# A decoder trunk's beginning: who asks for the first blocks, in what pieces, and how sums over partitions are taken

## The chip, the core and the metric

The kernel runs on one core of a Trainium2 chip. The core has a matrix engine (TensorE), two elementwise engines (VectorE, ScalarE), a general one (GpSimd) and SyncE, which here only asks for transfers. Sixteen DMA engines move data between the chip's main memory and the core's on-chip memory. The metric is the device time of one execution in microseconds, a median over runs. A trace of one profiled execution tells when each instruction began and ended.

## The reference

A trunk of two layers over a sequence of 1024 tokens with 1024 features, all in float32. The first layer normalises each token by the root mean square of its features, multiplies by `w_in_a` (1024 x 2560), applies a short causal convolution and two gates to the first 1280 columns, runs a linear recurrence over time, multiplies by the SiLU of the other 1280 columns, and projects back by `w_out_a`. The second layer is a multi-head latent attention (8 heads, causal) with its own projections. A last normalisation gives the output. Of this the change touches two kinds of work: the start of the first projection, and two of the normalisations' sums.

```
h = rms_norm(x, norm_a)          # y = x * rsqrt(mean(x*x) + eps) * g
u = h @ w_in_a                   # 1024 x 1024 by 1024 x 2560
...
return rms_norm(x, final_norm)
```

## The kernel before, in words

Features lie on the 128 partitions and tokens along the free dimension, so x is eight blocks (`k` = 0 to 7) of 128 features by 1024 tokens, and a product with a weight matrix adds eight matmuls over `k` into one bank of PSUM (128 x 512 values: one of 128 output columns, one half of the tokens).

Float32 products are made from rounded parts. `hl` (lines 80 to 83) writes `hi`, a copy rounded to the type fp32r, on ScalarE (L82), and `lo = src - hi` on VectorE (L83). `mm3` (lines 113 to 116) then issues three matmuls: hi·hi (L114), weight hi by data lo (L115), weight lo by data hi (L116). A float32 matmul without this splitting is possible as well; in the trace it is two instructions in place of one.

The normalisation is taken behind the product: x is multiplied by the gain while it is split (`xsplit`, L261 on ScalarE and L262 on VectorE), and the factor of each token is applied to the product later (`byr`, L162). That factor needs the sum of x*x over all features: `squares(k)` squares block `k` on ScalarE (L277 for block 0, L279 for the others) and adds it into `accp` on VectorE (L158, the last with L156). `accp` then holds 128 partial sums for each token; a matmul with a matrix of ones (`onesd`) sums them over the partitions (L140, in `rstd`), and `newton` (L148 to L151) makes the reciprocal root.

The beginning (lines 285 to 338) goes thus. Nine matmuls of ones by ones (`NWARM`, L287) keep TensorE working while the first data come. Within `manual_schedule` the instructions of SyncE, ScalarE and VectorE are executed in the order in which they are written; TensorE's order is made by a planner, which may put a matmul that it expects to be ready ahead of one that waits. SyncE asks for the vectors (`vec`: gains, biases and so on, L128), the first half of x's block 0, four blocks of the first weight column group `wina[0]`, the second half of x's block 0, four blocks of `wina[10]` (the gate's columns), and then whole blocks of x (L254 for x, L266 for weights). The raw weights have two buffers, so the second four blocks of each group are asked for when the first have been split. For each `k`, x is split, four groups of three matmuls follow (two column groups by two halves of tokens), and the squares of the block before are added (`SQL` = 1 block late). Before block 4 the second weights are split. When all blocks are through, the sums over partitions follow for the two halves, and the rest of the softplus (`step`, small VectorE operations) with them. Behind the block the loop over ten channel tiles begins, in which the planner orders all engines.

The end (lines 992 to 1058) makes the last projection in three chunks of tokens (512, 256, 256). For each of eight output blocks it multiplies, adds the residual (L1036), squares on ScalarE (L1038, L1041), and adds into `acc` (L156, L158). The sum of a chunk over partitions (`final`, L1005) and its normalisation and store (L1008, L1009) are written behind the second output block of the next chunk. The last chunk sums in its own way (L1044, L1045). Tiles with the tag `sq` have two buffers there.

Of the kernel before, what the change touches and what calls it, by code (L numbers as in the profile page):

```python
# [9 lines left out]
F32 = mybir.dt.float32  # L10
F32R = mybir.dt.float32r
# [7 lines left out]
D = 1024  # L19
# [25 lines left out]
PG1 = 1  # L45
CHUNKS = ((0, 512), (512, 256), (768, 256))
FINAL = ((0, 2, "sync"), (2, 4, "scalar"), (4, 6, "sync"), (6, 8, "scalar"))
NWARM = 9
SQL = 1
GADD = ()  # L50
NWA = 7
# [6 lines left out]
def trunk(tc, xT, wina, vecs, wgate, wouta, winc, wuk, wuv, wuq, wuqr, woutb, rope, outT):  # L58
# [12 lines left out]
    def nm(s):  # L71
        uid[0] += 1
        return f"{s}_{uid[0]}"
# [7 lines left out]
    def hl(src, hi, lo):  # L81
        A.activation(out=hi, in_=src, func=AF.Copy)  # L82
        V.tensor_tensor(out=lo, in0=src, in1=f(hi), op=ALU.subtract)  # L83
# [39 lines left out]
    def hs(h):  # L123
        return slice(h * HW, (h + 1) * HW)


    vec = con.tile([P, NVEC], F32, name="vec")
    nc.sync.dma_start(out=vec, in_=vecs)  # L128
    tiny = con.tile([P, 1], F32, name="tiny")
    V.memset(tiny, 1e-30)  # L130
    atab = con.tile([P, 1], F32, name="atab")
# [2 lines left out]
    onesr = con.tile([P, P], F32R, name="onesr")  # L134
    V.tensor_copy(out=onesr, in_=onesd)

    def rstd(acc_half, out, ps, inv, y, u, parts=None):

        if parts is None:
            T.matmul(out=ps, lhsT=onesd, rhs=acc_half, start=True, stop=True)  # L140
        else:
            hl(acc_half, *parts)
            T.matmul(out=ps, lhsT=onesr, rhs=parts[0], start=True, stop=False)
            T.matmul(out=ps, lhsT=onesr, rhs=parts[1], start=False, stop=True)
        newton(out, ps, inv, y, u)

    def newton(out, ps, inv, y, u):
        A.activation(out=y, in_=ps, func=AF.Abs_reciprocal_sqrt, scale=inv)  # L148
        A.activation(out=u, in_=y, func=AF.Square)
        V.scalar_tensor_tensor(out=u, in0=ps, scalar=inv, in1=u, op0=ALU.mult, op1=ALU.mult)  # L150
        V.scalar_tensor_tensor(out=out, in0=u, scalar=-3.0, in1=y, op0=ALU.add, op1=ALU.mult)  # L151
# [26 lines left out]
    def tt(dt=F32):  # L178
        return ta.tile([P, HW], dt, tag="t", bufs=14, name=nm("t"))

    def pst():
        return psp.tile([P, HW], F32, tag="ps", name=nm("ps"))
# [68 lines left out]
    def xload(k, c=slice(0, S)):  # L251
        if len(xrs) == k:
            xrs.append(page(F32))
        nc.sync.dma_start(out=xrs[k][:, c], in_=xT[:, k, c])  # L254
# [6 lines left out]
        A.activation(out=xh, in_=xrs[k][:, c], func=AF.Copy, scale=g)  # L261
        V.scalar_tensor_tensor(out=xl, in0=xrs[k][:, c], scalar=g, in1=f(xh), op0=ALU.mult, op1=ALU.subtract)  # L262

    def wraw(src, k0):
        raw = wp.tile([P, 4 * P], F32, tag="wr", bufs=2, name=nm("wr"))
        nc.sync.dma_start(out=raw, in_=src[:, k0 * P:(k0 + 4) * P])  # L266
        return raw

    def wsplit(raw, ks):
        hi = wp.tile([P, 4 * P], F32R, tag="wh", bufs=4, name=nm("wh"))  # L270
        lo = wp.tile([P, 4 * P], F32R, tag="wl", bufs=4, name=nm("wl"))
        hl(raw, hi, lo)
        ks += [(hi[:, k * P:(k + 1) * P], lo[:, k * P:(k + 1) * P]) for k in range(4)]

    def squares(k):
        if k == 0:
# [10 lines left out]
        T.matmul(out=warm[:, 0:P], lhsT=onesd, rhs=onesd, start=True, stop=True)  # L287
    rb = accp
    with tc.manual_schedule(engines={_E.SP, _E.Activation, _E.DVE}):
        A.activation(out=atab, in_=onesd[:, 0:1], func=AF.Abs_reciprocal_sqrt)  # L290
        sp = softplus()

        def step(n):
            for _ in range(n):
                next(sp, None)

        xload(0, hs(0))
        r = [wraw(wina[0], 0)]
        xload(0, hs(1))
        r.append(wraw(wina[NCT], 0))  # L300
        xload(1)
        xload(2)
        xload(3)
        step(SPN[0])
        xsplit(0, hs(0))
        wsplit(r[0], wx)
        xsplit(0, hs(1))
        wsplit(r[1], wg)
        r = [wraw(wina[0], 4), wraw(wina[NCT], 4)]
        for k in range(4, NKT):  # L310
            xload(k)
        ps0 = [pst() for _ in range(4)]

        def products(k):
            for i in range(4):
                mm3(ps0[i], (wx, wg)[i // 2][k], (xs[k][0][:, hs(i % 2)], xs[k][1][:, hs(i % 2)]), k == 0, k == NKT - 1)

        products(0)
        done = 0
        for k in range(1, NKT):  # L320
            xsplit(k)
            step(SPN[1])
            if k == 3:
                wsplit(r[0], wx)
                wsplit(r[1], wg)
            products(k)
            while done <= k - SQL:
                squares(done)
                step(SPN[1])
                done += 1  # L330
        for k in range(done, NKT):
            squares(k)
        ws = wload(wgate[0], 2 * P, tag="s", pool=ta, rb=1, hb=1)
        wx = wtile(wina[1], NKT, cast=True)
        for h in range(2):
            t1, t2 = tt(), tt()
            rstd(accp[:, hs(h)], rb[:, hs(h)], pst(), 1.0 / D, t1, t2)
        step(99)

    ys = []  # L340
# [661 lines left out]

    def final(c, n, x2s, acc):
        ps = pm()[:, 0:n]
        T.matmul(out=ps, lhsT=onesd, rhs=acc, start=True, stop=True)  # L1005
        root(n, ps, acc)
        for dt in range(NKT):
            V.scalar_tensor_tensor(out=x2s[dt], in0=x2s[dt], scalar=fn[:, dt:dt + 1], in1=acc, op0=ALU.mult, op1=ALU.mult)  # L1008
            nc.sync.dma_start(out=outT[dt, :, c], in_=x2s[dt])  # L1009
# [103 lines left out]
```

## Time and profile before

| | |
|---|---|
| median of 3 runs | 875.53 us (875.16 to 877.53) |
| the profiled execution | 874.77 us, its span 873.0 us |
| TensorE busy | 856.0 us, 98% of the span |
| VectorE busy | 658.6 us, 75% |
| ScalarE busy | 516.9 us, 59% |
| GpSimd busy | 73.2 us, 8% |
| granted TensorE clock, mean | 0.997 |

How to read the lines of the profile: a line of a timeline gives the start in the span, the duration (both us), the engine, the line of the kernel, the operation, what it writes and reads, shapes, a count if several like instructions are merged, and in brackets how long the engine was idle before it and who released it. PE is TensorE, PEld its weight load, DVE VectorE, ACT ScalarE, POOL GpSimd, and SPq or ACTq the issue of a transfer by SyncE or ScalarE. `ps`, `pm` are PSUM tiles, `pg` pages of on-chip memory, `wr`, `wh`, `wl` a weight raw, hi and lo. The chain of waits is followed back from the last instruction: its rows give start, length, and the engine and line that set the time there. Matmuls are pipelined, so a row's duration is longer than the distance to the next. A row of the windows view gives the stretch and its length, the busy time of each engine with the number of instructions (PE, PEld, DVE, ACT, POOL), the granted clock, the busy share of the DMA engines and GB/s. Times quoted from the trace are of the profiled execution.

### The profile page before, as it was taken

To read this page: it belongs to the slowest core of one execution; us is meant where nothing else is said; L and a number is where in the kernel's file an instruction comes from. 1 tells how busy PE (TensorE), PEld (TensorE's weight loads), DVE (VectorE), ACT (ScalarE), POOL (GpSimd) and SP (SyncE) were. 2 spreads that over 40 slices of the span, in tenths; PEclk is the share of its full clock that TensorE was granted. 3 is DMA by queue.
4 is the path that set the end of the run, shared out by engine and by line. 5 is a ranking of instruction groups with operands and counts; after the bars stand their busy time and mean duration, and the time that the engine had idled before them with its cause. 6 is when DMAs were issued, how large, how long until landed. Compare 5 with 4: busy or idle time off the path is not lost.

```text
span 873.0 us, 12178 instructions
## 1 busy us (share of the span) xinstructions
PE 856.0 (98%) x4326; PEld 728.2 (83%) x4326; DVE 658.6 (75%) x1222; ACT 516.9 (59%) x956; POOL 73.2 (8%) x143
## 2 busy tenths in 40 slices
PE   8999999999999999999999999999999999999995
PEld 6788888888887888888778888988998998888995
DVE  7888788777877764779988957887797887775453
ACT  7457777777787543699885545555565554431222
POOL 1000110011000100000211320000000000010000
PEclk9999999999999999999999999999999999999998
DMA  8333333333212544133535663222231326666032
GB/s 297 92 98 107 96 91 97 106 103 96 73 37 88 171 141 167 49 109 113 184 118 203 216 231 115 76 87 92 70 112 68 112 67 257 215 212 209 23 128 68
DMA packets 51789, 109.00 MB, mean 125 GB/s; under 512 B 6544, under 2 KB 16656, under 8 KB 51728
## 3 DMA queue, kind: packets, MB, share of 16 engines
q1 hardware_dynamic: 35968, 67.19, 24.2%
q0 software_dynamic: 15216, 40.51, 13.9%
q8 instruction: 34, 0.56, 0.3%
q10 hardware_dynamic: 544, 0.52, 0.2%
q14 instruction: 27, 0.22, 0.1%
HBM read 81.46 MB, written 26.21 MB: 123 GB/s over the span
## 4 chain that ended last, share of the span: by engine, by line
PE 78%; issue 8%; DVE 6%; ACT 4%; DMA 2%; POOL 1%; SPq 0%; DVEq 0%; POOLq 0%; ACTq 0%
PE ps L115 12%; PE ps L116 12%; PE ps L114 12%; PE pm L115 6%; PE pm L116 6%; PE pm L114 6%; PE pm L877 4%; PE pm L893 2%; PE pm L894 2%; PE s L858 2%; PE s L859 2%; PE s L857 2%; PE s L861 2%; PE s L860 2%; PE pm L892 2%
## 5 line engine op out<-in xcount | busy, mean ns | idle before, releaser
L114 PE MATMUL ps<-pg,wh 128*128 128x512 f32 x672 | 261.8, 391 | 3.8 <-DVE tk L627 1.4
L115 PE MATMUL ps<-pg,wh 128*128 128x512 f32 x672 | 261.9, 390 | 0.5 <-DVE pg L262 0.3
L116 PE MATMUL ps<-pg,wl 128*128 128x512 f32 x672 | 261.6, 390 | 0.1
L114 PEld LDWEIGHTS ps<-pg,wh 128*128 128x128 f32 x672 | 126.0, 188 | 31.9 <-DVE tk L627 1.8
L115 PEld LDWEIGHTS ps<-pg,wh 128*128 128x128 f32 x672 | 126.2, 188 | 28.0 <-DVE pg L262 1.4
L116 PEld LDWEIGHTS ps<-pg,wl 128*128 128x128 f32 x672 | 126.2, 188 | 27.1 <-DVE wl L83 1.0
L82 ACT ACTIVATE pt<-pm 128x512 fp32r<-128x512 f32 (+2 forms) x96 | 44.3, 490 | 59.1 <-PE pm L877 55.9
L867 ACT ACTIVATE pg<-s,m 128x128 f32<-128x128 f32 (+3 forms) x64 | 47.5, 742 | 48.0 <-DVE m L864 41.2
L114 PE MATMUL pm<-pg,pg 128*128 128x256 f32 (+1 forms) x192 | 61.9, 322 | 0.0
L115 PE MATMUL pm<-pg,pg 128*128 128x256 f32 (+1 forms) x192 | 61.6, 321 | 0.0
L116 PE MATMUL pm<-pg,pg 128*128 128x256 f32 (+1 forms) x192 | 61.4, 320 | 0.0
L83 DVE TENSOR_TENSOR pt<-pm,pt 128x512 fp32r<-128x512 f32 (+2 forms) x96 | 50.5, 546 | 2.2 <-ACT pt L82 2.1
L864 DVE TENSOR_REDUCE m<-s 128x1 f32<-128x128 f32 (+3 forms) x64 | 48.1, 753 | 1.0
L83 DVE TENSOR_TENSOR wl<-wr,wh 128x512 fp32r<-128x512 f32 (+2 forms) x57 | 32.7, 577 | 16.3 <-ACT wh L82 16.2
L358 DVE SCALAR_TENSOR_TENSOR t<-xb,vec,t 128x512 f32<-128x512 f32 x60 | 44.7, 745 | 0.4
L82 ACT ACTIVATE wh<-wr 128x512 fp32r<-128x512 f32 (+2 forms) x57 | 30.7, 543 | 22.8 <-PE ps L115 10.6
L82 ACT ACTIVATE pg<-pg 128x512 fp32r<-128x512 f32 x42 | 26.2, 631 | 29.8 <-DVE pg L412 18.4
L877 PE MATMUL pm<-ident,pg 128*128 128x128 f32 x288 | 42.3, 274 | 0.3 <-DVE pg L869 0.3
L115 PE MATMUL pm<-pg,wh 128*128 128x512 f32 x108 | 42.3, 392 | 0.0
L116 PE MATMUL pm<-pg,wl 128*128 128x512 f32 x108 | 42.3, 392 | 0.0
L114 PE MATMUL pm<-pg,wh 128*128 128x512 f32 x108 | 42.1, 390 | 0.0
L857 PE MATMUL s<-pg,pg 128*128 128x512 f32 (+2 forms) x96 | 37.2, 388 | 2.0 <-ACT pg L867 2.0
(222 smaller groups left out, 1785.7 us busy)
## 6 DMA issues: line engine op xcount, KB each, us to landing
wr<-wina SPq DMA_DIRECT2D x40, 256.0 KB, 2.9
wh<-wina POOLq DMA_DIRECT2D x36, 256.0 KB, 3.0
wa<-winc SPq DMA_DIRECT2D x24, 256.0 KB, 2.7
ysd<-pg POOLq DMA_DIRECT2D x12, 512.0 KB, 3.2
pg<-ysd SPq DMA_DIRECT2D x12, 512.0 KB, 8.4
wr<-wouta SPq DMA_DIRECT2D x16, 256.0 KB, 2.7
t<-xT SPq DMA_DIRECT2D x16, 256.0 KB, 4.1
x1d<-t POOLq DMA_DIRECT2D x16, 256.0 KB, 3.3
```

What stands on the lines that cost most here:

```text
L82: A.activation(out=hi, in_=src, func=AF.Copy)
L83: V.tensor_tensor(out=lo, in0=src, in1=f(hi), op=ALU.subtract)
L114: T.matmul(out=ps, lhsT=w[0], rhs=r[0], start=first, stop=False, skip_group_check=more)
L115: T.matmul(out=ps, lhsT=w[0], rhs=r[1], start=False, stop=False, skip_group_check=more)
L116: T.matmul(out=ps, lhsT=w[1], rhs=r[0], start=False, stop=last, skip_group_check=more)
L358: V.scalar_tensor_tensor(out=xc, in0=xb[:, j:j + HW], scalar=cwv[j], in1=xc, op0=ALU.mult, op1=ALU.add)
L857: T.matmul(out=sc[:, c], lhsT=q[0][:, ql], rhs=k[0][:, c], start=True, stop=False)
L858: T.matmul(out=sc[:, c], lhsT=q[0][:, ql], rhs=k[1][:, c], start=False, stop=False)
L859: T.matmul(out=sc[:, c], lhsT=q[1][:, ql], rhs=k[0][:, c], start=False, stop=False)
L864: V.tensor_reduce(out=m, in_=sc, axis=AX.X, op=ALU.max, negate=True)
L867: A.activation(out=p_[:, 0:nk], in_=sc, func=AF.Exp, bias=m, accum_out=l)
L877: T.transpose(out=ps[:, (b - b0) * P:(b - b0 + 1) * P], in_=p_[:, b * P:(b + 1) * P], identity=ident)
```

## The change

The vectors are asked for by ScalarE, as are the first two of eight blocks of the first weight groups (`load(0, 2, nc.scalar)`); SyncE asks for x's blocks 0 and 1 in halves, and then for weight blocks 2 and 3. ScalarE's small first activation, which brings its table with it, stands behind its three requests. Weights are split in pieces as they come: blocks 0 and 1 before block 0's matmuls, blocks 2 and 3 behind the split of x's block 1. The second four blocks of the weights, and x's blocks 4 to 7, are asked for behind that. Blocks 0 and 1 use `first(k)`, which issues for each half of the tokens the four products with x's hi part and then the two with its lo part. The squares of block 0 move behind the split of block 2. There are eight warm-up matmuls in place of nine. The sum of `accp` over partitions, and the sums in `final`, are made from `hi` and `lo` with `onesr` (ones in fp32r), two matmuls in place of one of float32; in `final` these two tiles take buffers of the tag `sq`.

```diff
-NWARM = 9
+NWARM = 8
...
-    nc.sync.dma_start(out=vec, in_=vecs)
+    nc.scalar.dma_start(out=vec, in_=vecs)
...
+    class Weights:
+        def __init__(self, src, ks):
+            self.src = src
+            self.raw = wp.tile([P, 4 * P], F32, tag="wr", bufs=2, name=nm("wr"))
+            self.hi = wp.tile([P, 4 * P], F32R, tag="wh", bufs=4, name=nm("wh"))
+            self.lo = wp.tile([P, 4 * P], F32R, tag="wl", bufs=4, name=nm("wl"))
+            ks += [(self.hi[:, k * P:(k + 1) * P], self.lo[:, k * P:(k + 1) * P]) for k in range(4)]
+        def load(self, k0=0, k1=4, q=nc.sync):
+            c = slice(k0 * P, k1 * P)
+            q.dma_start(out=self.raw[:, c], in_=self.src[:, c])
+        def split(self, k0=0, k1=4):
+            c = slice(k0 * P, k1 * P)
+            hl(self.raw[:, c], self.hi[:, c], self.lo[:, c])
...
-        A.activation(out=atab, in_=onesd[:, 0:1], func=AF.Abs_reciprocal_sqrt)
...
+        w0 = [Weights(wina[j][:, 0:4 * P], w) for j, w in ((0, wx), (NCT, wg))]
         xload(0, hs(0))
-        r = [wraw(wina[0], 0)]
+        for w in w0:
+            w.load(0, 2, nc.scalar)
         xload(0, hs(1))
-        r.append(wraw(wina[NCT], 0))
-        xload(1)
+        xload(1, hs(0))
+        xload(1, hs(1))
+        A.activation(out=atab, in_=onesd[:, 0:1], func=AF.Abs_reciprocal_sqrt)
+        for w in w0:
+            w.load(2, 4)
         xload(2)
         xload(3)
         step(SPN[0])
+        w0[0].split(0, 2)
         xsplit(0, hs(0))
-        wsplit(r[0], wx)
+        w0[1].split(0, 2)
         xsplit(0, hs(1))
-        wsplit(r[1], wg)
-        r = [wraw(wina[0], 4), wraw(wina[NCT], 4)]
-        for k in range(4, NKT):
-            xload(k)
...
+        def first(k):
+            for h in range(2):
+                for i in range(2):
+                    w, x = (wx, wg)[i][k], xs[k][0][:, hs(h)]
+                    T.matmul(out=ps0[2 * i + h], lhsT=w[0], rhs=x, start=k == 0, stop=False)
+                    T.matmul(out=ps0[2 * i + h], lhsT=w[1], rhs=x, start=False, stop=False)
+                for i in range(2):
+                    T.matmul(out=ps0[2 * i + h], lhsT=(wx, wg)[i][k][0], rhs=xs[k][1][:, hs(h)], start=False, stop=False)
-        products(0)
+        first(0)
+        xsplit(1, hs(0))
+        xsplit(1, hs(1))
+        for w in w0:
+            w.split(2, 4)
+        w4 = [Weights(wina[j][:, 4 * P:], w) for j, w in ((0, wx), (NCT, wg))]
+        for w in w4:
+            w.load()
+        for k in range(4, NKT):
+            xload(k)
+        first(1)
         done = 0
-        for k in range(1, NKT):
+        for k in range(2, NKT):
             xsplit(k)
             step(SPN[1])
             if k == 3:
-                wsplit(r[0], wx)
-                wsplit(r[1], wg)
+                for w in w4:
+                    w.split()
             products(k)
...
+        ap = [(tt(F32R), tt(F32R)) for _ in range(2)]
+        for h in range(2):
+            hl(accp[:, hs(h)], *ap[h])
         for h in range(2):
             t1, t2 = tt(), tt()
-            rstd(accp[:, hs(h)], rb[:, hs(h)], pst(), 1.0 / D, t1, t2)
+            ps = pst()
+            for i in range(2):
+                T.matmul(out=ps, lhsT=onesr, rhs=ap[h][i], start=i == 0, stop=i == 1)
+            newton(rb[:, hs(h)], ps, 1.0 / D, t1, t2)
...
     def final(c, n, x2s, acc):
         ps = pm()[:, 0:n]
-        T.matmul(out=ps, lhsT=onesd, rhs=acc, start=True, stop=True)
+        hi = td.tile([P, n], F32R, tag="sq", name=nm("ah"))
+        lo = td.tile([P, n], F32R, tag="sq", name=nm("al"))
+        hl(acc, hi, lo)
+        T.matmul(out=ps, lhsT=onesr, rhs=hi, start=True, stop=False)
+        T.matmul(out=ps, lhsT=onesr, rhs=lo, start=False, stop=True)
```

More of the change, by code (lines that the diff above doesn't have):

```diff
@@ L135, in trunk @@
     V.tensor_copy(out=onesr, in_=onesd)
[L137 to L145, printed above, removed]
     def newton(out, ps, inv, y, u):
@@ L262, in xsplit @@
         V.scalar_tensor_tensor(out=xl, in0=xrs[k][:, c], scalar=g, in1=f(xh), op0=ALU.mult, op1=ALU.subtract)
[L264 to L273, printed above, removed]
+    class Weights:
[11 more added lines that the diff above has]
+            hl(self.raw[:, c], self.hi[:, c], self.lo[:, c])
     def squares(k):
```

## The prediction

> **What bounds the kernel now.** I read the page first, for the bound of the whole.
>
> ```profile
> span 873.0 us, 12178 instructions
> PE 856.0 (98%) x4326; PEld 728.2 (83%) x4326; DVE 658.6 (75%) x1222; ACT 516.9 (59%) x956; POOL 73.2 (8%) x143
> ```
>
> TensorE is busy for 98% of the span, so a microsecond taken from its stream, or from a wait of its stream, comes off the end, and 17 us of waits are all there is to take. The profiled execution took 874.77 us (span 873.0 and 1.8 around it), 0.8 below the median of 875.53. So I work out differences on the trace and take them from the median. A difference below 0.3% (2.6 us) can't be told from none here.
>
> Next the chain of waits of the first 62 us: what holds TensorE at the beginning.
>
> ```profile
> 1.19 0.42 SPq L254
> ...
> 3.08 5.07 DMA pg<-xT
> ...
> 9.36 1.29 DVE pg L262
> 10.70 0.50 PE ps L115
> ...
> 29.54 1.72 PE ps L140 x4
> ```
>
> The second block of x lands at 8.15; its split on ScalarE and VectorE (9.36 + 1.29) lets TensorE go on at 10.70. From there the chain is TensorE alone, but the timeline shows that it has company. Of VectorE, ScalarE and TensorE:
>
> ```profile
> 4.26 0.72 ACT L261 ACTIVATE pg<-pg,vec 128x512 fp32r<-128x512 f32 x1 [2.03 <-DMA pg<-xT]
> ...
> 9.23 1.04 ACT L277 ACTIVATE accp<-pg 128x1024 f32<-128x1024 f32 x1
> 10.17 1.13 ACT L261 ACTIVATE pg<-pg,vec 128x1024 fp32r<-128x1024 f32 x1
> 11.21 1.04 ACT L279 ACTIVATE pg<-pg 128x1024 f32<-128x1024 f32 x1
> 11.34 1.28 DVE L262 SCALAR_TENSOR_TENSOR pg<-pg,vec,pg 128x1024 fp32r<-128x1024 f32 x1 [0.70 <-ACT pg L261]
> 12.16 1.14 ACT L261 ACTIVATE pg<-pg,vec 128x1024 fp32r<-128x1024 f32 x1
> 12.54 1.22 DVE L158 TENSOR_TENSOR accp<-accp,pg 128x1024 f32<-128x1024 f32 x1
> 13.20 1.14 ACT L82 ACTIVATE wh<-wr 128x512 fp32r<-128x512 f32 x2
> 13.68 1.28 DVE L262 SCALAR_TENSOR_TENSOR pg<-pg,vec,pg 128x1024 fp32r<-128x1024 f32 x1
> 14.88 1.28 DVE L83 TENSOR_TENSOR wl<-wr,wh 128x512 fp32r<-128x512 f32 x2
> ...
> 17.22 1.27 DVE L262 SCALAR_TENSOR_TENSOR pg<-pg,vec,pg 128x1024 fp32r<-128x1024 f32 x1
> 18.31 0.39 PE L114 MATMUL ps<-pg,wh 128*128 128x512 f32 x1
> 18.55 0.50 PE L115 MATMUL ps<-pg,wh 128*128 128x512 f32 x1
> ```
>
> VectorE runs without a pause from 11.34 to 18.49: the splits of blocks 2 and 3, two additions of squares (the second, at 16.08, in the rows left out), two weight remainders and the split of block 4. TensorE's first matmul on the remainder of block 4 (L115) starts at 18.55, right behind that split. So at 18.5 both chains arrive together, and a start that is earlier on TensorE alone meets VectorE there. This is the row that decides the change's first half.
>
> **The change: the beginning.** What sets VectorE's chain is the moment when ScalarE begins the split of block 2; call it T (10.17 now). What comes behind T changes too: now the square of block 0 (L277) lies ahead of T, in a pause, and afterwards it stands behind T, followed by the square of block 1. From the rows, ScalarE's starts follow one another by 1.04 (split), 0.95 (square) and 0.52 (weights). VectorE's split of block 2 starts at T + 1.17 as now; the addition of square 1 has to wait for ScalarE until T + 1.04 + 0.95 + 1.06 = T + 3.05; split 3 follows at T + 4.24, the remainders at T + 5.44, the second addition at T + 6.64, split 4 at T + 7.78. That is the present 17.22 for T = 9.44, and earlier only for an earlier T.
>
> T is the later of ScalarE being free and block 2 landing. Three stretches answer for the landing: the issues of blocks 1 to 3, the answer for the second of them alone (KB, us to landing), and the transfers by windows (GB/s at the end of each row).
>
> ```profile
> 3.08 1.45 SPq L254 DMA_DIRECT2D pg<-xT  x3
> pg<-xT SPq DMA_DIRECT2D x1, 512.0 KB, 5.9
> ...
> 2.00:4.50 2.50, 2.50 (x15) 2.50 (x15) 0.91 (x7) 0.46 (x3) 0.00 (x0) 1.00 0.88 207
> 4.50:8.00 3.50, 2.08 (x9) 1.04 (x8) 2.46 (x4) 2.41 (x4) 0.00 (x0) 1.00 1.03 395
> ```
>
> The three issues stand in 1.45 us, so block 2 is issued near 3.55 and lands at 9.45. The same 2.1 MB (three blocks of 512 KB, four quarters of weights of 128 KB, the vectors) have to arrive by then after the change, so at an unchanged rate T is 9.45 and the beginning gains nothing. But between 2 and 4.5 us the transfers ran at 207 GB/s, against 395 afterwards, and the change asks for x and the first weights from two engines, from 0.74 on: by 2.1 us for 1.08 MB (three halves of x, the vectors, two pieces), where now it is 0.57. If that fills the slow stretch, 2.5 us × 188 GB/s = 0.47 MB come earlier, worth 1.2 us at 395. ScalarE then becomes the bound: the first half of x lands at 4.26 now, four half splits of 0.72 and four pieces of weights at 0.33 (an estimate, half of the 0.57 of a whole and a little) make 4.2, so it is free at 8.5. T lies between 8.5 and 9.45; no row is nearer to one end, so I take the middle, 9.0, a gain of 0.45 on VectorE's chain. TensorE can add to that: when it waited for block 1 now, three hi·hi matmuls (L114) were put ahead of the first remainder.
>
> ```profile
> 9.74 0.84 PE L114 MATMUL ps<-pg,wh 128*128 128x512 f32 x3
> ```
>
> If the same is done at block 4, up to 3 × 0.225 = 0.7 more is saved (0.84 for three of which one takes 0.39: 0.225 apart). Starting near 6.1 (now 5.99) and with no stall, TensorE would come to block 4 at 6.1 + 48 × 0.225 = 16.9, not 18.31. So 1.4 is the ceiling; the floor is 0, or -0.5 if block 2 came half a microsecond later through sharing with the other queue. I take 0.8: the 0.45, and half of the 0.7.
>
> The Trainium skill speaks against this part ("DMA: Bandwidth & Descriptors", section "Issuing engines are not separate DMA queues"): transfers started by different engines run on the same 16 DMA engines and interleave, and only the sequencer's issue time is saved. Taken strictly it gives the first rival below; the row at 207 GB/s says that the early stretch isn't full, so I don't take it strictly.
>
> The other edits here cost nothing. The vectors are still asked for first; the first split needs them at 4.26, 1.5 after they land:
>
> ```profile
> 2.72 0.17 DVE L192 TENSOR_SCALAR sp<-vec 128x10 f32<-128x10 f32 x1 [1.13 <-DMA vec<-vecs]
> ```
>
> The table load (1.28 now at the head of ScalarE) comes behind three issues of some 0.45 there and is over at 3.6, before x lands; without that cover it would delay the first split one for one. The second weights and blocks 4 to 7 are issued behind the remainders (about 9), while blocks 2 and 3 still move; block 4 is wanted only at T + 6. One warm-up matmul less (NWARM) lies in time in which TensorE waits anyway:
>
> ```profile
> 1.09 3.77 PE L287 MATMUL ps<-onesd 128*128 128x128 f32 x18 [1.09 <-DVE onesd L133]
> 4.24 0.62 PE L287 MATMUL ps<-onesd 128*128 128x128 f32 x4
> 4.36 0.50 PE L287 MATMUL ps<-onesd 128*128 128x128 f32 x3
> 5.99 0.50 PE L114 MATMUL ps<-pg,wh 128*128 128x512 f32 x1 [1.13 <-ACT wh L82]
> ```
>
> Its instructions start 0.22 apart up to 4.24 and 0.12 apart after, so the faster pace came with two instructions to spare once the last two are gone.
>
> **The sum over partitions at 29 us.** L140's two f32 products are four instructions and take 1.72 (chain row above). Four on rounded parts at 0.225 take 0.9: 0.8 less. New are two copies on ScalarE and two subtractions on VectorE, 0.6 and 0.69 each (as the 0.57 of a copy above, and L98 here).
>
> ```profile
> 33.21 0.69 DVE L98 TENSOR_TENSOR wl<-wr,wh 128x512 fp32r<-128x512 f32 x1 [3.71 <-DMA wr<-wina]
> 33.82 0.68 DVE L150 SCALAR_TENSOR_TENSOR t<-ps,t 128x512 f32<-128x512 f32 x1
> 47.53 0.69 DVE L83 TENSOR_TENSOR t<-t,t 128x512 fp32r<-128x512 f32 x1
> 48.81 0.39 PE L114 MATMUL ps<-t,wh 128*128 128x512 f32 x1
> ```
>
> The subtractions fall in VectorE's pause (3.71 before 33.21, from 29.5 on) and are ready at 30.2 and 30.9, later than TensorE would want them (29.5). TensorE has the next channel tile's products to go on with, which need no sum, so I take no stall; without that cover it waits some 0.7 + 0.3, and the gain is gone. Who needs the result is late anyway: L150 at 33.82 stands behind L98, which waited for a transfer. Range -0.2 to 0.8. Both gains bring TensorE 1.6 earlier to the gate products of the second half (48.81), whose input L83 is ready at 48.22, 0.6 ahead; as VectorE comes forward by 0.45 only, 0.5 could be given back, unless other products go first. I put 0.3 against it: 0.5 is left.
>
> **The final sums.** From the chain and the timeline at the end:
>
> ```profile
> 821.01 0.86 PE pm L1005 x2
> 844.90 0.43 PE pm L1005 x2
> ...
> 816.74 0.69 DVE L158 TENSOR_TENSOR acc<-acc,sq 128x512 f32<-128x512 f32 x1 [0.76 <-ACT sq L1041]
> 821.57 0.42 ACT L1041 ACTIVATE sq<-x 128x256 f32<-128x256 f32 x1 [2.53 <-DVE x L1036]
> 845.37 0.39 ACT L148 ACTIVATE t<-pm 128x256 f32<-128x256 f32 x1 [1.89 <-PE pm L1005]
> 845.65 0.41 ACT L1041 ACTIVATE sq<-pg 128x256 f32<-128x256 f32 x1
> ```
>
> 0.86 becomes 2 × 0.225, 0.43 half of that: 0.4 and 0.2 less. Range 0.6 down to what rival 3 loses. The sum of the first chunk is complete at 817.4, and ScalarE has pauses until 821.57, so copy and subtraction (0.6 + 0.69) can be over by 819, before TensorE comes to them at 821.0. The last chunk's own sum (L1045) isn't touched. I take 0.6.
>
> Sum: 0.8 + 0.5 + 0.6 = 1.9; 875.5 - 1.9 = 873.6 (on the profiled execution 872.9).
>
> **The rivals.** (1) The transfers are the bound and T stays at 9.45: the beginning gives 0, the sums 0.5 + 0.6: 874.4. For it: 395 GB/s from 4.5 on. Against: the slow stretch before. (2) Everything counts, 1.4 + 0.8 + 0.6 = 2.8: 872.7. For it: hi·hi matmuls moved ahead at block 1. Against: the two chains meeting at 18.5. (3) Slower: the final sums wait. The copy of acc is written behind the next chunk's second square. If ScalarE executes it there (behind 821.57 + 0.42) and TensorE's sum stays behind the second product, then the remainder is ready at 822.0 + 0.6 + 0.69 = 823.3, and TensorE stands from 821.0 on: 2.3 lost less 0.4. In the next chunk the square ends at 846.06, copy and subtraction add 0.8, against 844.9: 2.0 lost less 0.2. Together +3.7, and with 1.3 gained before, +2.4: 877.9. It decides as soon as the copy lies behind that square. For it: the order of writing. Against: L148 of the same function ran ahead of the square (845.37 before 845.65), though written later. (4) The eight warm-up matmuls don't bring the fast pace; the first products then run 0.2 slower each until it comes, at most eight of them, 1.7, of which some 0.9 lies in the wait for block 4: the sum falls to 1.1: 874.4. The granted clock stood at 1.00 in every row, so the page can't tell. The Trainium skill ("TensorE: Matmul & The Clock Gate", section "What's actually happening") puts the change after about 3.4 us of sustained work, in a window that runs free; the rows agree with 3.15 (1.09 to 4.24).
>
> **How the numbers follow.** Forecast 0.47, rivals (1) 0.2, (2) 0.18, (3) 0.1, (4) 0.05. Faster by over 0.3% (below 872.9): most of (2), a fifth of the forecast: 0.26. Slower by over 0.3%: half of (3), and 0.04 for a reordering that no row here foretells: 0.09. Within: 0.65. The forecast's own range is 872.6 to 874.8; for 8 in 10 I take 872.0 to 876.5, from (2) with 0.8 of difference between executions to half of the way to (3).
>
> **What would show it.** Right: block 2's split on ScalarE begins near 9.0; the addition of square 1 waits for ScalarE; TensorE meets split 4 at about 17.5 to 18; four L140-like matmuls at 0.23 with no gap; the end's sums 0.45 and 0.24. Wrong: T at 9.4 or later, a gap of TensorE before the sums at 29, 821 or 845, or L114 starts 0.4 apart at 6 us.

## The result, and the profile after

The changed kernel takes 878.12 us (median of 19 runs, 877.14 to 878.9) against 875.8 for the kernel before, timed beside it (874.86 to 877.87). The ratio is 1.0024, with a 95% interval of 1.0018 to 1.0031: 2.1 us longer, 1.6 to 2.7. That is outside of the range given (872.0 to 876.5), on the slower side, and close to the 877.9 of rival (3), to which I gave a chance of 0.1. The profiled execution took 878.1 us, its span 876.3. The head of its page:

```profile
span 876.3 us, 12193 instructions
PE 855.2 (98%) x4324; PEld 728.0 (83%) x4324; DVE 661.7 (76%) x1229; ACT 519.2 (59%) x963; POOL 73.2 (8%) x143
```

TensorE is busy for 0.8 us less and the span is 3.3 longer: the stream of matmuls did become shorter, and waits came in that are worth more. The view of TensorE's waits (us in total, times, longest) says where; the rows that are new or longer at the beginning and at the end are these:

```profile
PE pm L1034 <- ACT ah L82: 2.8, 2, 1.5
...
PE ps L323 <- ACT pg L252: 1.7, 1, 1.7
...
PE ps L114 <- ACT pg L252: 0.6, 1, 0.6
...
PE ps L362 <- DVE t L83: 0.5, 1, 0.5
```

The first row is new and the largest of all: the matmul that sums a finished chunk over partitions (L1034, in `final`) waits twice for ScalarE's copy of `acc`. The others belong to the beginning and to the sum at 29 us. The chain of waits at the end (start, length, who sets the time):

```profile
822.27 0.42 ACT sq L1071
822.69 0.53 ACT ah L82
823.26 0.50 PE pm L1034
...
847.53 0.42 ACT sq L1071
847.95 0.32 ACT ah L82
848.30 0.39 PE pm L1034
...
869.73 0.69 DVE pg L1087
```

Before, these places were TensorE's own (L1005 at 821.01 and 844.90). Now TensorE stands both times behind a square on ScalarE, and only then comes the copy. The square of the chunk's last block, which goes before all this, is a place that both kernels have. In ScalarE's timeline of the kernel before, and in its chain (the first product of the last normalisation):

```profile
816.08 0.63 ACT L1041 ACTIVATE sq<-x 128x512 f32<-128x512 f32 x1 [4.81 <-DVE x L1036]
```

```profile
866.17 0.69 DVE pg L1057
```

and in the changed kernel's timeline, of the end and of the beginning:

```profile
4.02 0.17 DVE L183 TENSOR_SCALAR sp<-vec 128x10 f32<-128x10 f32 x1 [2.43 <-DMA vec<-vecs]
5.45 0.42 ACT L82 ACTIVATE wh<-wr 128x256 fp32r<-128x256 f32 x1 [1.79 <-DMA wr<-wina]
6.53 0.50 PE L323 MATMUL ps<-pg,wh 128*128 128x512 f32 x1 [1.66 <-ACT pg L252]
9.35 1.15 ACT L252 ACTIVATE pg<-pg,vec 128x1024 fp32r<-128x1024 f32 x1
10.89 1.84 SPq L245 DMA_DIRECT2D pg<-xT  x4
17.24 1.15 ACT L252 ACTIVATE pg<-pg,vec 128x1024 fp32r<-128x1024 f32 x1 [1.66 <-DMA pg<-xT]
18.42 1.28 DVE L253 SCALAR_TENSOR_TENSOR pg<-pg,vec,pg 128x1024 fp32r<-128x1024 f32 x1 [1.23 <-ACT pg L252]
30.16 0.77 PE L362 MATMUL ps<-t,onesr 128*128 128x512 f32 x2
30.63 1.29 DVE L83 TENSOR_TENSOR t<-accp,t 128x512 fp32r<-128x512 f32 x2
31.37 0.50 PE L362 MATMUL ps<-t,onesr 128*128 128x512 f32 x1 [0.45 <-DVE t L83]
...
816.79 0.63 ACT L1071 ACTIVATE sq<-x 128x512 f32<-128x512 f32 x1 [4.81 <-DVE x L1066]
```

From that square to the last normalisation it was 866.17 - 816.08 = 50.09 us and is 869.73 - 816.79 = 52.94: 2.85 more. The square itself comes 0.7 later than before. At the beginning, the first sum over partitions starts at 30.16, where it started at 29.37 in the timeline of before (the chain counts it from 29.54, where the matmul ahead of it ends). Block 2's split begins at 9.35 (10.17 before), but block 4's only at 17.24, behind a wait for its transfer, and VectorE's share of it is done 1.2 us later than before (18.42 against 17.22).

### The profile page after: what moved, and what is told of

Its sections match the earlier page's. It is cut to its first block, busy times and chain, and to the rows that moved or that the text cites. A ratio compares the mean times of both kernels' runs of the same rounds, so it can differ in the third digit from the quotient of the medians.

```text
span 876.3 us, 12193 instructions
## 1 busy us (share of the span) xinstructions
PE 855.2 (98%) x4324; PEld 728.0 (83%) x4324; DVE 661.7 (76%) x1229; ACT 519.2 (59%) x963; POOL 73.2 (8%) x143
## 4 chain that ended last, share of the span: by engine, by line
PE 68%; issue 10%; DVE 9%; ACT 8%; DMA 3%; POOL 1%; DVEq 0%; ACTq 0%; POOLq 0%; SPq 0%
PE ps L116 9%; PE ps L115 9%; PE ps L114 9%; PE pm L116 6%; PE pm L115 6%; PE pm L114 6%; PE pm L903 3%; PE pm L920 2%; PE pm L919 2%; PE s L884 2%; PE s L883 2%; PE s L885 2%; PE s L887 2%; PE s L886 2%; PE pm L918 2%
## 5 line engine op out<-in xcount | busy, mean ns | idle before, releaser
L114 PE MATMUL ps<-pg,wh 128*128 128x512 f32 x664 | 257.8, 390 | 3.3 <-DVE tk L653 1.3
L115 PE MATMUL ps<-pg,wh 128*128 128x512 f32 x664 | 258.6, 390 | 0.4 <-DVE pg L253 0.3
L116 PE MATMUL ps<-pg,wl 128*128 128x512 f32 x664 | 258.3, 389 | 0.1
L114 PEld LDWEIGHTS ps<-pg,wh 128*128 128x128 f32 x664 | 124.4, 188 | 30.6 <-DVE tk L653 1.7
L115 PEld LDWEIGHTS ps<-pg,wh 128*128 128x128 f32 x664 | 124.6, 188 | 27.4 <-DVE pg L253 1.0
```

Of the source, the lines that this page charges most:

```text
L114: T.matmul(out=ps, lhsT=w[0], rhs=r[0], start=first, stop=False, skip_group_check=more)
L115: T.matmul(out=ps, lhsT=w[0], rhs=r[1], start=False, stop=False, skip_group_check=more)
L116: T.matmul(out=ps, lhsT=w[1], rhs=r[0], start=False, stop=last, skip_group_check=more)
```

## The experiments

Each was timed in five rounds against the kernel before on the same chip. Differences in us are the ratio less one, times 875.5.

**The two halves apart.** The first kernel is the one before, with only the new `final` in it; the second is the changed kernel with only the buffers of `final` renamed.

```diff
 # kernel before
-        T.matmul(out=ps, lhsT=onesd, rhs=acc, start=True, stop=True)
+        hi = td.tile([P, n], F32R, tag="sq", name=nm("ah"))
+        lo = td.tile([P, n], F32R, tag="sq", name=nm("al"))
+        hl(acc, hi, lo)
+        T.matmul(out=ps, lhsT=onesr, rhs=hi, start=True, stop=False)
+        T.matmul(out=ps, lhsT=onesr, rhs=lo, start=False, stop=True)
```

> The kernel before with only the sums of final() made from rounded parts, in buffers of the tag sq. Theory W (the sums wait: the copy of acc lies behind the next chunk's second square on ScalarE): slower than before by 2.0 to 2.9 us, with two gaps of TensorE near 822 and 846, about 1.5 us each. Theory S (the sums gain 0.6 and the whole loss comes from the beginning): faster by 0.6.

```diff
 # changed kernel
-        hi = td.tile([P, n], F32R, tag="sq", name=nm("ah"))
-        lo = td.tile([P, n], F32R, tag="sq", name=nm("al"))
+        hi = td.tile([P, n], F32R, tag="t1", name=nm("ah"))
+        lo = td.tile([P, n], F32R, tag="t2", name=nm("al"))
```

> The changed kernel, with the rounded parts in final() taken from the tags t1 and t2 in place of sq, nothing else. Theory B (the parts stand behind the square because they share its two buffers): the copies move ahead of the square, the gaps of TensorE go, 3.0 to 3.5 us faster than the changed kernel, 874.7 to 875.2. Theory O (the order of writing puts them there): no difference, 878.

The new `final` alone: 878.26 us against 875.44, 1.0032 [1.002, 1.0044], 2.8 us more. The changed kernel with other buffers: 874.41, 0.9987 [0.9978, 0.9996], 1.1 less than before. So this one part makes the whole loss, and the tag alone decides it: with other tags and the same order of writing the loss is gone, which leaves out the theory that the order puts the copy behind the square. In the groups by form of the first kernel (busy time and mean ns; then idle time ahead), each chunk waits once:

```profile
L1008 PE MATMUL pm<-ah,onesr 128*128 128x512 f32 x1 | 0.5, 497 | 1.5 <-ACT ah L82 1.5
...
L1008 PE MATMUL pm<-ah,onesr 128*128 128x256 f32 x1 | 0.4, 385 | 1.3 <-ACT ah L82 1.3
```

and in the second kernel's timeline and chain:

```profile
816.21 0.63 ACT L1071 ACTIVATE sq<-x 128x512 f32<-128x512 f32 x1 [4.81 <-DVE x L1066]
817.66 0.63 ACT L82 ACTIVATE ah<-acc 128x512 fp32r<-128x512 f32 x1 [0.82 <-DVE acc L149]
...
822.14 0.41 ACT L1071 ACTIVATE sq<-x 128x256 f32<-128x256 f32 x1
```

```profile
821.14 0.23 PE pm L1034
821.37 0.23 PE pm L1035
...
865.71 0.69 DVE pg L1087
```

Written at the same place, the copy now runs at 817.66, in the pause where I had put it, 4.5 us ahead of the next chunk's second square. The two matmuls of the first chunk's sum take 0.23 each without a wait, and the stretch to the last normalisation is 865.71 - 816.21 = 49.50: 0.59 less than before, the 0.6 of the forecast. The stretch is the same in every profile of its kind: 50.09 with float32 sums (four profiles), 52.94 to 52.96 with the tag `sq` (three), 49.50 with other tags (seven). With the tag `sq` the copies shared two buffers with the squares of the next chunk. That the tag holds them back is shown; that it does so by the turns of the buffers is my reading, and by which of the two tiles (the buffer for `lo` would be the one which the second square fills) wasn't tried. The 1.1 of the whole isn't the sum of its parts as they measure below (0.4 and 0.2 less, 0.3 more); the intervals, some 0.8 to either side each, allow for both.

**The sums one by one.** The kernel before with `final` in the buffers `t1` and `t2`, and the kernel before with only the sum at 29 us from rounded parts:

```diff
 # kernel before
+        ap = [(tt(F32R), tt(F32R)) for _ in range(2)]
+        for h in range(2):
+            hl(accp[:, hs(h)], *ap[h])
...
-            rstd(accp[:, hs(h)], rb[:, hs(h)], pst(), 1.0 / D, t1, t2)
+            ps = pst()
+            for i in range(2):
+                T.matmul(out=ps, lhsT=onesr, rhs=ap[h][i], start=i == 0, stop=i == 1)
+            newton(rb[:, hs(h)], ps, 1.0 / D, t1, t2)
```

> The kernel before with only the sums of final() from rounded parts, in the tags t1 and t2. By the sum of the prediction: 0.6 faster than before (two float32 products of 0.86 and 0.43 halve). Rival: extra work on ScalarE and VectorE delays the chunk's outputs and takes it back: no difference.

> The kernel before with only the sum at 29 us from rounded parts. By the prediction's optimistic term: 0.8 faster (no stall); by its other bound (TensorE waits 0.7 + 0.3 for the two remainders): 0.2 slower to no difference. The changed kernel's trace, with a wait of 0.45, speaks for 0 to 0.4 faster.

`final`: 875.32 against 875.57, 0.9995 [0.9986, 1.0004]; the forecast 0.6 lies within, and its trace has the same 49.50 us, but by time it can't be told from nothing. The sum at 29 us: 875.58, 0.9998 [0.9989, 1.0007]. There the first matmul runs and the other three wait for the remainder; in the changed kernel two run before the wait:

```profile
29.46 0.40 PE L342 MATMUL ps<-t,onesr 128*128 128x512 f32 x1
30.24 1.10 PE L342 MATMUL ps<-t,onesr 128*128 128x512 f32 x3 [0.39 <-DVE t L83]
```

**The beginning.** The changed kernel with both sums as before; and the changed kernel with block 4 of x asked for right behind block 3, ahead of the remainders of the first weights:

```diff
 # changed kernel
         xload(3)
+        xload(4)
...
-        for k in range(4, NKT):
+        for k in range(5, NKT):
```

> The changed kernel with both kinds of sums over partitions as before (float32 ones), so that only the beginning is changed. Theory L (block 4 of x is asked for 2 us later and lands at 17.2 in place of 13.3; TensorE's first products end 0.8 later): slower than before by 0.6 to 0.9. Theory G (the beginning gains, as forecast): faster by 0.8.

> The changed kernel with x's block 4 asked for behind block 3, ahead of the second weights, nothing else. Theory L: block 4 lands by 13, VectorE's split of it starts near 17.2 in place of 18.4, and the kernel is 0.9 to 1.3 us faster than the changed kernel. Theory Q (the transfers are the bound, the second weights come as much later as block 4 comes earlier): within 0.3 of the changed kernel.

The beginning alone: 875.83 against 875.44, 1.0003 [0.9995, 1.0012]: 0.3 us more, from 0.4 less to 1.1 more. The forecast's 0.8 less is outside. Block 4 early: 878.13, 1.0031 [1.002, 1.0043], no better than the change, though VectorE's split of block 4 starts at 17.14 there, where the first theory had it. In that profile the first products ran at half the pace for some microseconds, which I had not expected (below), so this run alone can't clear or blame block 4. Thirteen warm-up matmuls were tried with the good buffers, without and with block 4 early, and in the kernel before:

```diff
 # changed kernel, final in t1 and t2
-NWARM = 8
+NWARM = 13
```

> The changed kernel with the rounded parts of final() in buffers of their own (as in the second run) and thirteen warm-up matmuls in place of eight. Theory C (in most executions TensorE falls back to half its pace because it idles some 2 us between the warm-up and the first data, and starts block 4 late for it): first products 0.23 apart from the start, products end 0.5 to 1.0 earlier, 873.4 to 873.9 where 8 warm-ups gave 874.4. Theory D (block 4's transfer and VectorE set the beginning, the pace is covered): no difference, 874.4.

> As the run before, with x's block 4 asked for behind block 3 as well. Theory C with L (each of the two costs something only when the other is out of the way): products end near 28.9, 1.0 to 1.6 faster than 874.4. Theory D without L: 874.4; D with L: 0.5 to 1.2 faster than the run before.

> The kernel before with thirteen warm-up matmuls in place of nine, nothing else. Theory P (the kernel before also runs its first products at half pace in many executions, and loses 0.6 to 1.6 by it, as its products ended at 29.4 to 31.0 in four profiles): 0.4 to 1.0 faster than before, and products ending near 29.4. Rival (the wait for block 1 and VectorE cover it): no difference.

874.57 against 875.57 without block 4 early, 0.9987 [0.9978, 0.9996], the same as with eight: theory D, in which the pace is covered. With block 4 early 873.78, 0.9979 [0.997, 0.9988]: 0.7 us less by the ratios, though the intervals overlap. In the kernel before thirteen give 875.05 against 875.31, 0.9998 [0.9989, 1.0007]: no difference, as the rival had it.

**Who asks.** The best kernel so far (thirteen warm-up matmuls, block 4 early, `final` in `t1` and `t2`), with every first request from SyncE, the pieces unchanged:

```diff
 # kernel with thirteen warm-ups and block 4 early
-    nc.scalar.dma_start(out=vec, in_=vecs)
+    nc.sync.dma_start(out=vec, in_=vecs)
...
-            w.load(0, 2, nc.scalar)
+            w.load(0, 2)
```

> The sixth run's kernel (final() in buffers of its own, 13 warm-ups, block 4 early) with the vectors and the first weight pieces asked for by SyncE too, in the same pieces, in the order vectors, first half of x, pieces, second half. Theory K (two engines asking at once share the transfers, which makes the vectors and the first pieces later: 4.0 and 5.4 in place of 2.7 and about 4.7): vectors at 2.7, TensorE's first product 0.5 to 1.0 earlier than 6.67, the end equal or up to 0.5 faster, 873.3 to 873.8. Theory M (asking from two engines is what pays): everything about 0.5 later, 874.3.

875.39 against 875.31, 1.0001 [0.9992, 1.001], 1.9 us more than with two engines asking, and the intervals touch at no point. So asking from two engines pays, and more than the second theory gave it. The transfers from 4 to 6 us by windows (stretch, length, clock, share, GB/s), first with two engines, then with SyncE alone:

```profile
4.00:5.00 1.00, 1.00 1.02 368
5.00:6.00 1.00, 1.00 1.03 386
```

```profile
4.00:5.00 1.00, 1.00 0.64 150
5.00:6.00 1.00, 1.00 0.82 266
```

and ScalarE's timeline around block 2's split, in the same order:

```profile
9.90 1.15 ACT L252 ACTIVATE pg<-pg,vec 128x1024 fp32r<-128x1024 f32 x1 [0.51 <-DMA pg<-xT]
```

```profile
4.39 0.42 ACT L82 ACTIVATE wh<-wr 128x256 fp32r<-128x256 f32 x1 [2.16 <-DMA wr<-wina]
...
11.74 1.15 ACT L252 ACTIVATE pg<-pg,vec 128x1024 fp32r<-128x1024 f32 x1 [1.82 <-DMA pg<-xT]
```

With SyncE alone ScalarE starts earlier (4.39), and block 2 comes 1.8 us later. The issues of the halves of x, first with two engines (all four), then with SyncE alone (the last three):

```profile
0.74 1.83 SPq L245 DMA_DIRECT2D pg<-xT  x4
```

```profile
2.60 1.38 SPq L245 DMA_DIRECT2D pg<-xT  x3
```

The same seven requests (vectors, two pieces, four halves) are out at 2.57 with two engines, ScalarE's three included, and at 3.98 with one: 1.4 us later, which is most of the 1.8.

**Two wholes.** The kernel with block 4 early, with the remainders for the sum at 29 us written ahead of the next weights; and the same kernel with the beginning of before (requests, pieces and order):

```diff
 # kernel with block 4 early
+        ap = [(tt(F32R), tt(F32R)) for _ in range(2)]
+        for h in range(2):
+            hl(accp[:, hs(h)], *ap[h])
         ws = wload(wgate[0], 2 * P, tag="s", pool=ta, rb=1, hb=1)
         wx = wtile(wina[1], NKT, cast=True)
-        ap = [(tt(F32R), tt(F32R)) for _ in range(2)]
-        for h in range(2):
-            hl(accp[:, hs(h)], *ap[h])
```

> The sixth run's kernel with the rounded parts of the sum at 29 us ahead of the next weights' remainders on VectorE. Theory V (the sum gains nothing since its remainders stand behind 1.7 us of weight remainders): the wait of 0.45 before the third of the four products goes, 0.4 to 0.8 faster than 873.8. Rival: the weight remainders, 1.3 later, hold the next products by the same: no difference, or up to 0.5 slower.

> The kernel before, with its own beginning (requests, pieces, order), thirteen warm-up matmuls, and both sums on rounded parts in the forms that did not wait: the remainders for the sum at 29 us written ahead of the next weights, the final's parts in tags t1 and t2. The whole that has the changed beginning beside the same sums was 0.9975 of the kernel before (some 2.2 us less). Theory B: the changed beginning, with block 4 asked for early, is worth the 0.8 of my sum; then this kernel takes about 1.4 less than the kernel before (0.9984) and its first products end about 0.8 later than 28.99 of that whole. Theory N: the beginning is worth nothing; then this kernel is 2.2 less (0.9975), the two sums carry the whole. A ratio of 0.9990 or above says that the beginning carries more than half.

The first takes 873.11 against 875.31, 0.9975 [0.9965, 0.9984]: 2.2 us less than before, by the ratios 4.3 less than the change, and the best of all. Its waits of TensorE up to 40 us are one row, the start itself:

```profile
PE ps L285 <- DVE onesd L133: 1.1, 1, 1.1
```

The wait in the sum is gone, and the sum starts at 28.99 (block 2's split on ScalarE, block 4's on VectorE, the sum):

```profile
9.52 1.16 ACT L252 ACTIVATE pg<-pg,vec 128x1024 fp32r<-128x1024 f32 x1 [0.16 <-DMA pg<-xT]
...
17.28 1.28 DVE L253 SCALAR_TENSOR_TENSOR pg<-pg,vec,pg 128x1024 fp32r<-128x1024 f32 x1
...
28.99 1.00 PE L363 MATMUL ps<-t,onesr 128*128 128x512 f32 x3
```

By time, the step from 0.9979 to 0.9975 is inside the intervals. With the old beginning 874.88 against 875.9, 0.9987 [0.9978, 0.9996]: 1.1 us less. That is near the 0.9984 of the theory in which the beginning is worth 0.8, and the 0.9975 of the other lies just outside of its interval; in its profile the sum starts at 30.30, 1.3 later than 28.99. But the two wholes differ by 1.1 with intervals of some 0.8 on either side, so what the beginning is worth there (with block 4 early and thirteen warm-ups) stays open between nothing and some 2 us.

## Why the prediction was wrong

**The final sums: the step that failed.** I took 0.6, because "ScalarE has pauses until 821.57", so that copy and subtraction "can be over by 819". The pauses are there and are long enough; the kernel with other buffers uses them just so and gains the 0.6 in its trace. What the step left out is that a tile in the tag `sq` isn't written in a pause: with that tag the copy runs behind the square (822.69), with another in the pause (817.66). I read that as turns in two buffers, shared with the squares. Rival (3) had the place and the effect right (the copy behind the square at 822.27 + 0.42, a matching wait in the next chunk), but not the reason: it laid the copy there by the order of writing, which is the same in the kernel where the copy runs ahead. Its price was 3.7; measured are 2.85 in the trace and 2.8 by time. It was oversized where I let the sum wait for the remainder too: TensorE waited 1.54 for the copy alone, and the product with `hi` covered part of the subtraction. That its 877.9 lies so near to the measured 878.1 is luck: the price was 0.9 too high, and the 1.3 of gains that it set against it can't be seen in the runs of those parts. I gave it 0.1 on the ground that "L148 of the same function ran ahead of the square". But L148 writes a tile of another tag, so that row said nothing on the point; the sentence in my own description that the tag has two buffers was the one to follow.

**The beginning: a term of 0.8 that measured as 0.3 the other way (-0.4 to 1.1).** Thirteen profiles together (all but the one with every request from SyncE) say which of its parts held. T is the start of block 2's split on ScalarE, S that of block 4's on VectorE, E the end of the first products (the start of the first sum); us from the span's start, in each row the profiles in the same order.

| beginning | T | S | S - T | E - S |
|---|---|---|---|---|
| as before, 6 profiles | 10.17, 10.80, 11.06, 10.26, 11.10, 11.13 | 17.22, 17.85, 18.10, 17.29, 18.14, 18.17 | 7.03 to 7.05 | 12.15, 12.10, 12.86, 12.17, 12.17, 12.13 |
| changed, 4 profiles | 9.35, 9.88, 9.22, 10.39 | 18.42, 17.64, 16.98, 18.14 | 9.07, 7.76, 7.76, 7.75 | 11.74, 12.42, 12.92, 11.73 |
| changed, block 4 early, 3 profiles | 9.40, 9.90, 9.52 | 17.14, 17.66, 17.28 | 7.74, 7.76, 7.76 | 13.50, 11.77, 11.71 |

(As before: that kernel, new `final` alone, `final` with other buffers, the sum at 29 us alone, thirteen warm-ups, both sums. Changed: that kernel, other buffers, beginning alone, thirteen warm-ups. Early: block 4 early, the same with other buffers and thirteen warm-ups, the remainders first.)

The chain that I worked out, split 4 at T + 7.78, is right to 0.04 in six of seven: VectorE does set the pace there, and the square that moved behind T costs 0.73 against the old 7.05. (By its own rows the chain makes T + 7.73: 3.05 and the 1.14 from an addition to the next split are 4.19, where I wrote 4.24.) T was the term that failed, twice. I took 9.0; it never came below 9.22, and is 9.71 in the mean of four. The slow stretch that was to be filled did fill in part. In the changed kernel, for the same windows as in the prediction:

```profile
2.00:4.50 2.50, 2.50 (x14) 2.50 (x13) 0.45 (x5) 1.49 (x2) 0.00 (x0) 1.00 0.91 289
4.50:8.00 3.50, 1.84 (x8) 1.08 (x8) 2.37 (x7) 2.49 (x5) 0.00 (x0) 1.00 1.04 380
```

That is 289 GB/s where it was 207, but not 395, and 380 behind it: some 0.15 MB more by 8 us, where I had 0.47. And ScalarE, which I had free at 8.5, begins its work at 5.45 and not at 4.26, as its first work is now a piece of weights that lands only then; its 3.9 us of work, for which I had 4.2, end at 9.35. In the profiles with T at 9.88 and 10.39 it waits for block 2's transfer besides (0.62 and 1.16). And the T to compare it with was an early draw: 10.17 in the profile of before is the earliest of six, whose mean is 10.75. So T gained 1.04 in the mean, and 0.3 of that is left after the extra square. The "half of the 0.7" for hi·hi matmuls put ahead at block 4 held: three of them run there (18.44 in the changed kernel), and E - S is 0.4 shorter, 11.73 where it was 12.13, in the profiles that ran at full pace throughout.

So some 0.7 should be left, and the profiles show two things that use it up there, both of which I had put at nothing. One is block 4: "the second weights and blocks 4 to 7 are issued behind the remainders (about 9), while blocks 2 and 3 still move". SyncE's waits up to 32 us, in the changed kernel:

```profile
SPq L267 <- DVE wl L83: 2.9, 1, 2.9
...
SPq L267 <- DMA vec<-vecs: 0.9, 1, 0.9
SPq L245 <- DMA wr<-wina: 0.6, 1, 0.6
```

2.9 us go by before the remainders of the first weights are done, the request for block 4's group begins at 10.89 (8.74 before), and by then nothing moves. From the windows (engines, clock, share, GB/s at the end):

```profile
9.00:10.00 1.00, 1.00 (x6) 0.83 (x5) 1.00 (x4) 1.00 (x3) 0.00 (x0) 1.00 0.45 180
10.00:11.00 1.00, 1.00 (x6) 0.82 (x5) 0.81 (x3) 1.00 (x2) 0.00 (x0) 1.00 0.01 4
```

In the profile of the change this made block 4 the bound (S - T is 9.07, 1.3 too much), which is 0.3 in the mean of the four; in the other three it came just in time. It isn't the whole story, then, but a risk that asking early takes away. The other is the half pace of the first products (below): E - S is 0.7 to 1.8 larger in three of the seven, and in one of the six with the old beginning. Over the four profiles of the changed beginning E is 30.0 in the mean, where six with the old one have 30.06: nothing gained, as the time of the beginning alone says. By time neither of the two is shown: block 4 early with eight warm-ups gained nothing (1.0031 beside 1.0024), nor did thirteen warm-ups alone. With both E is 29.43 and 28.99, and the kernels are 0.7 and 1.1 us faster than with thirteen warm-ups and block 4 late (E 29.87); the second of them has lost its wait in the sum as well. As the intervals overlap, this is a reading that fits and not one that is shown, and where the 0.8 went stays open.

**Two engines asking.** That the early stretch wasn't full was right: from SyncE alone the same pieces moved at 150 and 266 GB/s where two engines had 368 and 386, and cost 1.9 us. Rival (1), an unchanged rate, falls with it as a mechanism, though its T of 9.45 was nearer than my 9.0. The Trainium skill ("DMA: Bandwidth & Descriptors", "Issuing engines are not separate DMA queues") says that asking from several engines saves the sequencer's issue time alone, and that this is usually small beside the transfer. The runs don't go against that: the 1.4 us by which the requests were out sooner is most of the 1.8 by which block 2 came sooner. What failed is my strict reading, in which issue time was worth nothing. The requests on ScalarE had a price that I put at nothing: the vectors land at 4.02 instead of 2.72 and ScalarE's first work is at 5.45 instead of 4.26.

**The sum at 29 us: 0.5 less forecast, 0.2 less measured (from 1.0 less to 0.6 more).** By time the forecast isn't refuted; in the trace the gain is gone. The cover that I named ("the next channel tile's products to go on with") isn't there. TensorE stood 0.45 at 31.37, for a remainder at 30.63 that came behind the next weights' remainders on VectorE. The distance from the sum's first matmul to the product behind its last is 1.72 in the kernel before (29.37 to 31.32, less 0.23 for a product in between) and 1.72 with only this sum changed (29.46 to 31.18). That is the case without cover that I had named: the 0.8 of the matmuls is used up, though not the 0.7 + 0.3 that I gave for it. With the old beginning and the sum's remainders written ahead of the next weights' it is 1.01 (30.30 to 31.31, no wait); that kernel, with both sums in the forms that don't wait, takes 1.1 less than before (0.4 to 1.9), which is the 0.5 and 0.6 of the forecast.

**Warm-up, rival (4).** The half pace that it feared came in some executions, in the form that it gave (in the kernel with the beginning alone, for the first eight products); but it came in two of four profiles with nine warm-up matmuls and in three of four with eight, so it doesn't hang on the one matmul less alone. With thirteen it is in no profile, and they changed no time that could be measured (0.9987 beside 0.9987, and 0.9998). What it costs on average is left open within those intervals. These intervals, some 0.1% to either side, also show that the 0.3% which I took for the smallest visible difference was too wide.

## What to carry to other kernels

Before a temporary is put in an existing small tag, follow its buffers' turns: the instruction that fills it can be held behind the other user of the tag, however long the pauses on its engine are; a tag of its own turned 2.1 us of loss into 1.1 of gain here. A beginning that is read from one profiled execution may be an early or a late draw: here block 2's split started anywhere between 10.17 and 11.13 with the same requests in the same order, so a forecast of less than a microsecond needs several profiles of it, and is best made as a difference between two points of one chain, which held to 0.04.

## What the runs showed of the hardware beside that

The half pace: in the kernel with the new `final` alone, whose beginning is that of before, the first products stand 0.43 us apart, where the usual distance is 0.23.

```profile
6.86 0.63 PE L115 MATMUL ps<-pg,wh 128*128 128x512 f32 x1
7.29 0.64 PE L116 MATMUL ps<-pg,wl 128*128 128x512 f32 x1
```

The granted clock read 1.00 there, while in the run with block 4 early, whose products also stood 0.43 apart, it read 0.50:

```profile
9.00:10.00 1.00, 1.00 (x4) 0.80 (x3) 1.00 (x3) 1.00 (x3) 0.00 (x0) 0.50 1.02 406
```

It was seen in five of eight profiles with eight or nine warm-up matmuls and in none of six with thirteen. In two of the five, the one above and the one of the beginning alone, it was there from the first product on, the clock read 1.00, and the warm-up matmuls before it had stood 0.21 apart to the last, which I read as a fast pace that had not come yet. In the other three the first products ran at full pace and then fell, the clock read 0.50, and the pauses of TensorE ahead of it were of half a microsecond to two. The remaining three of the eight had pauses of 0.8 to 1.7 without it. In the run with the beginning alone it lasted from 6.39 to 9.92, 3.5 us. The Trainium skill ("TensorE: Matmul & The Clock Gate", "What's actually happening") has the fast state after about 3.4 us of sustained work, which agrees with that length; it has the slow one come after an idle window of the same length, and here the pauses were shorter.

Some of SyncE's requests wait for an earlier transfer into another tile: the rows above name 0.9 us until `vec` had landed, which ScalarE had asked for, ahead of a request for weights, and 0.6 us for a piece of weights ahead of a request for a block of x. Why they wait isn't shown. And the rate of the transfers varies: between 11 and 15 us the kernel before ran at 348 to 422 GB/s in its profile, the same beginning with the new `final` at 258 to 315, and the changed kernel at 205 to 320. A pause of the transfers isn't the whole cause, since with block 4 early and no pause it was 250 to 344; the cause stays open, and the spread of T between executions may come from it.
